# Modulations, weight splits, the experts' gate and the bias rows in a kernel of two stacked blocks

## The chip, the cores and the metric

The kernel runs on one core of one Trainium2 chip. The metric is the device time of one execution in microseconds, the median of the runs.

## The reference, cut to what matters

Two blocks run one after the other over 256 tokens of width 1024, in fp32. In the first block each of two layers takes six modulations (shift, scale and gate, twice) from a conditioning vector, the latent attention two more.

```python
# first block, per layer
sh1, sc1, g1, sh2, sc2, g2 = jnp.split(c_act @ w_mod[layer] + b_mod[layer], 6, axis=-1)
h = modulate(rmsnorm(x, norm_g[layer]), sh1, sc1)
x = x + g1 * mix(h)            # forgetting attention in layer 0, latent attention in layer 1
h = modulate(rmsnorm(x, ffn_norm_g[layer]), sh2, sc2)
x = x + g2 * grouped_moe(h)    # sum over e of combine[:, e] * (silu(h @ w_gate[e]) * (h @ w_up[e])) @ w_down[e]

# second block, four layers: retention, MoBA, differential, retention
x = x + mixer(_rmsnorm(x, norm1[i]))      # MoBA and differential add rel_bias[bucket(distance)] to the scores
u = jax.nn.relu(_rmsnorm(x, norm2[i]) @ w_up[i]); x = x + (u * u) @ w_down[i]
```

## The kernel before

Every product of a weight is made of three matmuls on a high and a low part. `unit` loads 1 MiB of a weight into one of five `raw` buffers (SP's queue, L136), and for each half ACT copies the high part `wh` (L149) and another engine subtracts it to get the low part `wl` (L155). Six half units of `wh` and `wl` exist at a time, so splits run at most six ahead of PE. The subtracting engine is DVE, but in the forgetting attention it is GpSimd (POOL) for all 34 half units, by `SPL`.

The stages follow each other: an opening (constants, the first two modulations), forgetting attention (44 to 236 us), experts of layer 0 (to 502), latent attention (to 690), experts of layer 1 (to 950), then the second block: retention, four perceptrons, MoBA, differential attention, and a second retention at the end. A scheduler orders the instructions of each engine by the order of the code and by what is ready; every engine then works its list in order. `issue_after` adds an edge on one engine, and `HOLD` uses it: after so many splits of a stage, further splits may not come ahead of the step in `last` on DVE. For the first retention it is 2.

A modulation is a product of the conditioning vector `c` with 1024x1024 of `w_mod`. It is done in four steps of a load and four DVE instructions each, one multiply (L813) or multiply-adds (L815), that accumulate 128 partial rows in `macc`, 512 columns wide; eight matmuls with ones (L826) sum the partitions. Two modulations belong to the opening, twelve are put into later stages: `spare()` takes steps from a queue at places in the code, their number set by `PLAN0`, `PLAN1` and `MF`.

An expert's output is gathered as `dv`, two parts again: ACT multiplies by the combine weight (L1398), DVE makes the low part (L1399), and PE spreads it back to the tokens (L1409). The gate is applied behind the last expert, four multiplies and four adds on DVE (L908, L909). Then `norm_x` takes the root mean square of `x` (squares on ACT, L278; root steps on DVE, L255 to L265; `diag`, L879), and every engine passes a branch (L1248) that isn't taken here.

The attentions of the second block read a relative bias from `bias_rows` in DRAM, sixteen heads of 128 equal rows of 384. `spread_bias` writes them with DMAs from DRAM to DRAM, four issues of four heads each on ACT's queue in the first retention, behind the second head's first square (L496, L590). In that stage `rv` (L469) and `rg` (L471) scale what PE has projected, on ACT.

Of the kernel before, what the change touches and what calls it, by code (L numbers as in the profile page):

```python
# [31 lines left out]
GE = 4  # L32
HOLD = dict(ret0=2, mlp0=2, mlp1=2, mlp2=2, mlp3=2, moba=4)
SPL = {'fgt': (1, 0)}
# [6 lines left out]
PLAN1 = [1, 1, 1, 3, 0, 0, 2, 0, 1, 1, 1, 1, 0, 2, 0, 2]  # L41
# [43 lines left out]
class Net:  # L85
    def __init__(self, ctx, tc, I, C, out):
# [5 lines left out]
        self.last = None  # L92
# [38 lines left out]
    def load(self, ap, k, n):  # L131
        raw = self.raw.tile([128, UNIT], F32, name="raw", tag="raw")
        rv = raw[:, :k * n].rearrange("p (k n) -> p k n", k=k)
        aps = [ap] if len(ap.shape) == 3 else [ap[:, m] for m in range(ap.shape[1])]
        for m, a in enumerate(aps):
            self.nc.sync.dma_start(rv[:, m * a.shape[1]:(m + 1) * a.shape[1]], a)  # L136
        return rv

    def unit(self, ap, k, n):
# [4 lines left out]
        for k0 in range(0, k, step):  # L144
# [4 lines left out]
            nc.scalar.copy(h[:, :m * n], p)  # L149
# [4 lines left out]
            with self.tc.issue_after(self.last) if self.last and self.nsplit > HOLD.get(self.ph, 99) else nullcontext():  # L154
# [113 lines left out]
    def rstd(self, srcs, n):  # L268
# [5 lines left out]
        for i, pieces in enumerate(srcs):  # L274
            for j, p in enumerate(pieces):
                junk = self.jk.tile([128, 512], F32, name="junk", tag="junk")
                w = p.shape[-1]
                nc.scalar.activation(junk[:, :w], p, AF.Square, scale=n ** -0.5, accum_out=ss[:, i, j:j + 1])  # L278
# [25 lines left out]
    def add_x(self, acc, scale=None):  # L304
# [9 lines left out]
        self.last = i.ins  # L314
# [17 lines left out]
    def heads(self, proj, mix, wo, gate=None):  # L332
# [5 lines left out]
        def add(xs, ps, g):  # L338
# [4 lines left out]
            self.last = nc.vector.tensor_tensor(xs, ps, xs, OP.add).ins  # L343
# [37 lines left out]
    def _mlp(self, i):  # L381
# [52 lines left out]
    def _retention(self, i, j):  # L434
# [41 lines left out]
        def mix(h, q, k, v, g):  # L476
# [11 lines left out]
            for tok in range(NT):  # L488
# [7 lines left out]
                mid = nc.scalar.activation(junk, po, AF.Square, scale=rt, accum_out=ss)  # L496
                if i == 0 and h == 1 and tok == 0:
                    with self.tc.issue_after(mid.ins):
                        self.spread_bias()
# [86 lines left out]
    def spread_bias(self):  # L586

        d = self.dist
        for g in range(4):
            self.nc.scalar.dma_start(self.bias[4 * g:4 * g + 4, :, 0:384],  # L590
                                     bass.AP(tensor=d.tensor, offset=d.offset + g * 4 * 384,
                                             ap=[[384, 4], [0, 128], [1, 384]]))
# [162 lines left out]

    def rope(self):
# [39 lines left out]

    def mod(self, w, c0, bias, gain=None):
# [6 lines left out]
        def step(u):  # L804
            half = u // 2
            r = self.load(self.rows(w, u % 2 * 4, 4, c0 + half * 512, 512), 4, 512)
            if u % 2 == 0:
                spot["acc"] = self.mods.tile([128, 512], F32, name="macc", tag="macc")
            acc = spot["acc"]
            for k in range(4):  # L810
                kk = u % 2 * 4 + k
                if kk == 0:
                    i = nc.vector.tensor_scalar(acc, r[:, k, :], self.c[:, 0:1], None, op0=OP.mult)  # L813
                else:
                    i = nc.vector.scalar_tensor_tensor(acc, r[:, k, :], self.c[:, kk:kk + 1], acc, op0=OP.mult,  # L815
                                                       op1=OP.add)
            with self.tc.issue_after(i.ins):
                self.finish()
            if u % 2:
                self.finish = lambda: total(acc, slice(4 * half, 4 * half + 4))  # L820

        def total(acc, c):
            self.finish = lambda: None
            ps = self.pat()
            for f in range(4):
                nc.tensor.matmul(ps[:, f:f + 1], acc[:, f * 128:f * 128 + 128], self.ones[:, 0:1], start=True, stop=True)  # L826
            self.mark = nc.vector.tensor_tensor(col[:, c], ps[:, 0:4], bias[:, c], OP.add).ins
            if gain is not None:
                nc.vector.scalar_tensor_tensor(col[:, c], col[:, c], 1.0, gain[:, c], op0=OP.add, op1=OP.mult)
# [3 lines left out]
    def gate(self, col):  # L833

        nc = self.nc
        self.finish()
# [5 lines left out]
        for half in range(2):  # L842
# [5 lines left out]
            nc.scalar.copy(g[:, half * 512:half * 512 + 512], ps)  # L848
        return g
# [767 lines left out]
```

## Time and profile before

| what | value |
|---|---|
| time, median of 3 runs | 2425.5 us (2424.55 to 2428.33) |
| time of the profiled execution | 2425.37 us |
| its span | 2423.6 us |
| PE busy | 2250.8 us (93%) |
| DVE busy | 1309.7 us (54%) |
| ACT busy | 990.5 us (41%) |
| POOL busy | 92.3 us (4%) |

The shares are means over stages with different limits. The line of 40 slices and the table by stretch tell which engine is full where, a wait names the instruction that an engine stood before and the one that it waited for, and the rows of a line give the price of one instruction. A row of an engine's sequencer (ACTq, SPq) shows the time that an issue of a DMA held its queue.

### The profile page before, as it was taken

To read this page: it belongs to the slowest core of one execution; us is meant where nothing else is said; L and a number is where in the kernel's file an instruction comes from. 1 tells how busy PE (TensorE), PEld (TensorE's weight loads), DVE (VectorE), ACT (ScalarE), POOL (GpSimd) and SP (SyncE) were. 2 spreads that over 40 slices of the span, in tenths; PEclk is the share of its full clock that TensorE was granted. 3 is DMA by queue.
4 is the path that set the end of the run, shared out by engine and by line. 5 is a ranking of instruction groups with operands and counts; after the bars stand their busy time and mean duration, and the time that the engine had idled before them with its cause. 6 is when DMAs were issued, how large, how long until landed. Compare 5 with 4: busy or idle time off the path is not lost.

```text
span 2423.6 us, 34244 instructions
## 1 busy us (share of the span) xinstructions
PE 2250.8 (93%) x13738; PEld 1769.9 (73%) x13738; DVE 1309.7 (54%) x2594; ACT 990.5 (41%) x1622; POOL 92.3 (4%) x46
## 2 busy tenths in 40 slices
PE   4898999969989997979999999999999999999999
PEld 3787443348964332868799898998888998787987
DVE  7867211178841113645655664655786556665554
ACT  3444211146631112434444465444574445443443
POOL 1443000000000000000000000000000000000000
PEclk9888999989989998989999999999999999999999
DMA  9767899966679996445555543655534555454552
GB/s 308 245 212 282 345 375 416 388 209 226 232 290 416 410 400 254 161 157 174 159 189 191 183 131 100 196 182 171 188 124 139 197 186 187 154 176 143 188 174 88
DMA packets 264391, 541.96 MB, mean 224 GB/s; under 512 B 15752, under 2 KB 158720, under 8 KB 250912
## 3 DMA queue, kind: packets, MB, share of 16 engines
q1 hardware_dynamic: 252208, 528.84, 61.6%
q10 hardware_dynamic: 12016, 10.85, 1.4%
q8 instruction: 111, 1.82, 0.3%
q14 instruction: 56, 0.46, 0.1%
HBM read 538.57 MB, written 4.22 MB: 224 GB/s over the span
## 4 chain that ended last, share of the span: by engine, by line
PE 52%; DVE 5%; ACT 1%; ACTq 1%; issue 1%; DMA 0%; DVEq 0%
DVE wl L155 2%; ACTq L590 1%; ACT wh L149 1%; DVE rsa L261 0%; DVE rsy L265 0%; DVE xg L217 0%; PE acc__mlp__19994 L201 0%; PE acc__mlp__13136 L201 0%; PE acc__mlp__16583 L199 0%; PE acc__mlp__13134 L201 0%; PE acc__mlp__19992 L201 0%; PE acc__mlp__9856 L200 0%; PE acc__mlp__16583 L200 0%; PE acc__mlp__9856 L199 0%; PE acc__mlp__19995 L200 0%
## 5 line engine op out<-in xcount | busy, mean ns | idle before, releaser
L155 DVE TENSOR_TENSOR wl<-raw,wh 128x1024 fp32r<-128x1024 f32 (+2 forms) x492 | 575.7, 1190 | 393.4 <-ACT wh L149 390.7
L149 ACT CAST wh<-raw 128x1024 fp32r<-128x1024 f32 (+4 forms) x526 | 523.3, 1020 | 472.2 <-issue 58.0
L815 DVE SCALAR_TENSOR_TENSOR macc<-raw,c,macc 128x512 f32<-128x512 f32 x196 | 169.7, 866 | 4.2 <-DMA raw<-in_w_mod_dram 1.5
L155 POOL TENSOR_TENSOR wl<-raw,wh 128x1024 fp32r<-128x1024 f32 (+1 forms) x34 | 82.0, 2435 | 136.5 <-ACT wh L149 136.5
L400 ACT CAST aTh<-rl 128x512 fp32r<-128x512 f32 x56 | 34.8, 621 | 78.3 <-DVE rl L398 78.3
L537 ACT ACTIVATE p<-p,m 128x128 f32<-128x128 f32 (+1 forms) x128 | 56.9, 447 | 23.1 <-DVE m L535 22.8
L278 ACT ACTIVATE junk<-x 128x512 f32<-128x512 f32 x52 | 32.7, 630 | 66.6 <-DVE x L343 36.5
L401 DVE TENSOR_TENSOR aTl<-rl,aTh 128x512 fp32r<-128x512 f32 x56 | 38.8, 693 | 38.5 <-ACT aTh L400 38.5
L398 DVE TENSOR_TENSOR rl<-rl 128x512 f32<-128x512 f32 x56 | 38.4, 685 | 0.0
L261 DVE SCALAR_TENSOR_TENSOR rsa<-rsy,rsh 128x1 f32<-128x1 f32 x186 | 34.4, 215 | 2.6
L220 ACT CAST hTh<-xg 128x512 fp32r<-128x512 f32 (+1 forms) x36 | 21.3, 606 | 25.7 <-DVE xg L217 25.6
L1173 POOL TENSOR_TENSOR hTl<-xg,hTh 128x512 fp32r<-128x512 f32 x8 | 10.1, 1278 | 471.1 <-ACT xg L1172 471.1
L265 DVE SCALAR_TENSOR_TENSOR rsy<-rsa,rsy 128x2 f32<-128x2 f32 (+2 forms) x141 | 22.6, 160 | 3.2
L537 ACT ACTIVATION_READ_ACCUMULATOR p<-p,m 128x1 f32 x128 | 24.1, 188 | 0.0
L221 DVE TENSOR_TENSOR hTl<-xg,hTh 128x512 fp32r<-128x512 f32 (+1 forms) x36 | 23.4, 671 | 1.0 <-ACT hTh L220 0.7
L1409 PEld LDWEIGHTS acc__moe__2360<-dv,back 64*128 64x128 f32 x32 | 5.6, 183 | 17.8 <-ACT dv L1398 10.4
L1409 PE MATMUL acc__moe__2360<-dv,back 64*128 64x512 f32 x32 | 14.8, 476 | 3.5 <-ACT dv L1398 3.2
L1409 PEld LDWEIGHTS acc__moe__6273<-dv,back 64*128 64x128 f32 x32 | 5.5, 183 | 16.6 <-ACT dv L1398 8.7
L1409 PE MATMUL acc__moe__6273<-dv,back 64*128 64x512 f32 x32 | 14.4, 476 | 2.8 <-ACT dv L1398 2.4
L535 DVE TENSOR_SCALAR m<-m 128x2 f32<-128x2 f32 x64 | 16.6, 259 | 0.5
L826 PE MATMUL at__latpre__4176<-ones,macc 128*128 128x1 f32 x8 | 1.8, 351 | 16.0 <-DVEq L1248 16.0
L813 DVE TENSOR_SCALAR macc<-raw,c 128x512 f32<-128x512 f32 x28 | 15.5, 553 | 1.5 <-DMA raw<-in_w_mod_dram 1.5
(3933 smaller groups left out, 7333.2 us busy)
## 6 DMA issues: line engine op xcount, KB each, us to landing
raw<-in_w_up_dram SPq DMA_DIRECT2D x64, 1024.0 KB, 5.4
raw<-in_w_down_dram SPq DMA_DIRECT2D x64, 1024.0 KB, 4.9
raw<-in_w_mod_dram SPq DMA_DIRECT2D x48, 1024.0 KB, 5.2
raw<-in_ret_w_in_dram SPq DMA_DIRECT2D x48, 1024.0 KB, 5.2
raw<-in_exp_w_gate_dram SPq DMA_DIRECT2D x40, 1024.0 KB, 10.3
raw<-in_exp_w_down_dram SPq DMA_DIRECT2D x34, 1024.0 KB, 9.9
raw<-in_exp_w_up_dram SPq DMA_DIRECT2D x30, 1024.0 KB, 10.5
wh<-in_exp_w_up_dram SPq DMA_DIRECT2D x34, 512.0 KB, 11.3
```

What stands on the lines that cost most here:

```text
L149: nc.scalar.copy(h[:, :m * n], p)
L155: eng.tensor_tensor(l[:, :m * n], p, h[:, :m * n].bitcast(F32), OP.subtract)
L221: nc.vector.tensor_tensor(lo[:, k0:k0 + n, tok * 128:tok * 128 + 128], pv, d.bitcast(F32), OP.subtract)
L261: nc.vector.scalar_tensor_tensor(a[:, c], y[:, c], h[:, c], y[:, c], op0=OP.mult, op1=OP.mult)
L278: nc.scalar.activation(junk[:, :w], p, AF.Square, scale=n ** -0.5, accum_out=ss[:, i, j:j + 1])
L398: nc.vector.tensor_tensor(rl, rl, rl, OP.mult)
L400: nc.scalar.copy(h, rl)
L401: nc.vector.tensor_tensor(aT[1][:, 2 * j:2 * j + 2, :].rearrange("p k t -> p (k t)"), rl, h.bitcast(F32), OP.subtract)
L537: nc.scalar.activation(p[:, m, :], p[:, m, :], AF.Exp, bias=mx[:, m:m + 1], accum_out=rs[:, m, s:s + 1])
L590: self.nc.scalar.dma_start(self.bias[4 * g:4 * g + 4, :, 0:384], bass.AP(tensor=d.tensor, offset=d.offset + g * 4 * 384, ap=[[384, 4], [0, ...
L815: i = nc.vector.scalar_tensor_tensor(acc, r[:, k, :], self.c[:, kk:kk + 1], acc, op0=OP.mult, op1=OP.add)
L1409: mm(acc[tok][half], back[c, e % 4, tok * 128:tok * 128 + 128], dv[j][c, :], start=e == 0 and j == 0, stop=e == 15 and j == 1)
```

## The change

1. Opening: each step of a modulation loads two rows of 1024 columns, PE multiplies them in four matmuls (into four quarters of the partitions), and DVE copies or adds one 128x512. Eight small matmuls with a constant `pick` sum up. The reordering of the queue goes.
2. Later modulations stay on DVE, 1024 columns wide: eight instructions each where there were sixteen.
3. `SPL` is empty: the 34 splits of the forgetting attention go to DVE.
4. `HOLD` becomes 0 for the first retention and is new, 0, for the latent stage. ACT's copies are held too, and `last` after `norm_x` is the pair of the last `diag` on DVE and the last square on ACT.
5. The gate is folded into each expert: DVE multiplies by combine weight and gate from PSUM, ACT copies the high part, DVE subtracts. The gate is laid out ahead of the first expert (`gate_halves`), and behind the last only four adds are left. `PLAN1` ends with 3 in place of 2.
6. `spread_bias` moves to the first perceptron, eight issues of two heads on SP's queue, each behind the newest weight load.

```diff
-GE = 4
-HOLD = dict(ret0=2, mlp0=2, ...)
-SPL = {'fgt': (1, 0)}
+HOLD = dict(ret0=0, latpre=0, mlp0=2, ...)
+SPL = {}
...
-            nc.scalar.copy(h[:, :m * n], p)
...
-            with self.tc.issue_after(self.last) if self.last and self.nsplit > HOLD.get(self.ph, 99) else nullcontext():
+            hold = self.last if self.nsplit > HOLD.get(self.ph, 99) else ()
+            with ExitStack() as e:
+                for i in hold:
+                    e.enter_context(self.tc.issue_after(i))
+                nc.scalar.copy(h[:, :m * n], p)
                 eng.tensor_tensor(l[:, :m * n], p, h[:, :m * n].bitcast(F32), OP.subtract)
...
             down(c, prev)
+            if i == 0:
+                with self.tc.issue_after(self.loaded):
+                    self.spread_bias(c)
...
-        for g in range(4):
-            self.nc.scalar.dma_start(self.bias[4 * g:4 * g + 4, :, 0:384],
...
+        self.nc.sync.dma_start(self.bias[2 * g:2 * g + 2, :, 0:384],
+                               bass.AP(tensor=d.tensor, offset=d.offset + g * 2 * 384, ap=[[384, 2], [0, 128], [1, 384]]))
...
+            r = self.load(self.rows(w, 2 * u, 2, c0, 1024), 2, 1024)
+            if u == 0:
+                spot["acc"] = self.mods.tile([128, 1024], F32, name="macc", tag="macc")
             acc = spot["acc"]
+            if side:
+                ps = self.pat()
+                for k in range(2):
+                    for half in range(2):
+                        j = 32 * (2 * k + half)
+                        nc.tensor.matmul(ps[j:j + 32, :], self.c[:, 2 * u + k:2 * u + k + 1].to_broadcast([128, 32]),
+                                         r[:, k, half * 512:half * 512 + 512], start=True, stop=True)
+                if u == 0:
+                    i = nc.vector.tensor_copy(acc[:, 0:512], ps)
                 else:
+                    i = nc.vector.tensor_tensor(acc[:, 0:512], ps, acc[:, 0:512], OP.add)
+            else:
+                for k in range(2):
...
+    def gate_halves(self, col):
...
+        g = self.mods.tile([128, D], F32, name="gate", tag="gate", bufs=1)[:, 0:512]
+        ps = self.pat()
+        for half in range(2):
+            for k in range(4):
+                kk = half * 4 + k
+                nc.tensor.matmul(ps[half * 64:half * 64 + 64, k * 128:k * 128 + 128],
+                                 self.ident[0:8, kk:kk + 1].to_broadcast([8, 64]), row, start=True, stop=True)
+        nc.scalar.copy(g, ps)
...
+        self.last = (i.ins, self.sq)
...
-            nc.scalar.mul(dv[0], ps, cs)
-            nc.vector.scalar_tensor_tensor(dv[1], ps, cs, dv[0].bitcast(F32), op0=OP.mult, op1=OP.subtract)
+            t = self.wk.tile([128, 512], F32, name="dg", tag="dg", bufs=1)
+            nc.vector.scalar_tensor_tensor(t, ps, cs, gates, op0=OP.mult, op1=OP.mult)
+            nc.scalar.copy(dv[0], t)
+            nc.vector.tensor_tensor(dv[1], t, dv[0].bitcast(F32), OP.subtract)
...
-        self.add_gated(acc, G)
+        self.add_x(acc)
         self.norm_x()
```

The first place is DVE's list behind the second layer's experts, where `x` has been added up, down to the branch. `var` to `rsy` are the root's steps, `wl` the first splits of the retention. Before, a part of it:

```order
L909 TENSOR_TENSOR x<-x,xg 128x512 x2
L155 TENSOR_TENSOR wl<-raw,wh 128x1024 x2
L281 SCALAR_TENSOR_TENSOR var<-ss 128x2
L155 TENSOR_TENSOR wl<-raw,wh 128x1024
L255 TENSOR_SCALAR rsy<-var 128x2
L257 TENSOR_SCALAR rsh<-var 128x2
L155 TENSOR_TENSOR wl<-raw,wh 128x1024
L256 TENSOR_SCALAR rsy<-rsy 128x2
L155 TENSOR_TENSOR wl<-raw,wh 128x1024
L261 SCALAR_TENSOR_TENSOR rsa<-rsy,rsh 128x1 x2
L155 TENSOR_TENSOR wl<-raw,wh 128x1024
```

After the change this chain holds no split; one stands behind `diag`, and the others behind the branch. The second root of the same stage, from which `rv` is made, then stands so on DVE:

```order
L157 TENSOR_TENSOR wl<-raw,wh 128x1024
L283 SCALAR_TENSOR_TENSOR var<-ss 128x2
L157 TENSOR_TENSOR wl<-raw,wh 128x1024
L257 TENSOR_SCALAR rsy<-var 128x2
L259 TENSOR_SCALAR rsh<-var 128x2
L157 TENSOR_TENSOR wl<-raw,wh 128x1024
L258 TENSOR_SCALAR rsy<-rsy 128x2
L157 TENSOR_TENSOR wl<-raw,wh 128x1024
L263 SCALAR_TENSOR_TENSOR rsa<-rsy,rsh 128x1 x2
L157 TENSOR_TENSOR wl<-raw,wh 128x1024
L267 SCALAR_TENSOR_TENSOR rsy<-rsa,rsy 128x2
L157 TENSOR_TENSOR wl<-raw,wh 128x1024
```

Six splits stand between `var` and the last step there, where two stood before.

The second place is the bias rows. Before, on ACT in the first retention, between a head's square and the next head's scaling:

```order
L149 CAST wh<-raw 128x1024 x5
L496 ACTIVATE junk,oss<-at__ret__8754,rsy 128x512
L590 DMA bias_rows<-bias_by_distance 512x1x384 x4
L469 ACTIVATE rv<-pj__ret__8837,rsy 128x512
L149 CAST wh<-raw 128x1024
```

After, on SP in the first perceptron, two of eight chunks:

```order
L135 DMA raw<-in_w_down_dram 128x2x1024 x2
L591 DMA bias_rows<-bias_by_distance 256x1x384
L135 DMA raw<-in_w_up_dram 128x8x256 x2
L135 DMA raw<-in_w_down_dram 128x2x1024 x2
L591 DMA bias_rows<-bias_by_distance 256x1x384
L135 DMA raw<-in_w_up_dram 128x8x256 x2
```

One issue now follows each pair of `w_down` loads, and the next pair of `w_up` loads is queued behind it.

The third place is DVE in the forgetting attention, between the first and the second group of heads (`o` and `aTl` are the first group's result, `b` the second group's decay). Before:

```order
L221 TENSOR_TENSOR aTl<-at__fgt__678,aTh 128x2x128
L827 TENSOR_TENSOR mod<-at__fgt__752,vcols 128x4
L813 TENSOR_SCALAR macc<-raw,c 128x512
L815 SCALAR_TENSOR_TENSOR macc<-raw,c,macc 128x512 x7
L827 TENSOR_TENSOR mod<-at__fgt__831,vcols 128x4
L813 TENSOR_SCALAR macc<-raw,c 128x512
L815 SCALAR_TENSOR_TENSOR macc<-raw,c,macc 128x512 x7
L827 TENSOR_TENSOR mod<-at__fgt__911,vcols 128x4
L813 TENSOR_SCALAR macc<-raw,c 128x512
```

After:

```order
L157 TENSOR_TENSOR wl<-raw,wh 128x1024
L568 TENSOR_TENSOR o<-at__fgt__668,rs 128x256
L833 SCALAR_TENSOR_TENSOR macc<-raw,c,macc 128x1024
L223 TENSOR_TENSOR aTl<-at__fgt__678,aTh 128x2x128
L850 TENSOR_TENSOR mod<-at__fgt__750,vcols 128x8
L157 TENSOR_TENSOR wl<-raw,wh 128x1024
L831 TENSOR_SCALAR macc<-raw,c 128x1024
L833 SCALAR_TENSOR_TENSOR macc<-raw,c,macc 128x1024 x5
L850 TENSOR_TENSOR mod<-at__fgt__898,vcols 128x8
L833 SCALAR_TENSOR_TENSOR macc<-raw,c,macc 128x1024
```

The splits stand among the modulations' instructions now, where POOL had a list of its own; fewer and wider instructions accumulate the modulations.

## Rows read from the trace of the kernel before

**Rows 1.** The page's line of PE's busy tenths in 40 slices of the span.

```profile
PE   4898999969989997979999999999999999999999
```

**Rows 2.** Table by stretch: us, busy us and instructions by engine, clock, DMA share, GB/s.

```profile
15.00:43.00 28.00, 7.83 (x33) 7.25 (x34) 23.59 (x42) 1.99 (x2) 2.92 (x2) 1.00 1.06 374
60.00:240.00 180.00, 156.50 (x1179) 146.66 (x1179) 137.77 (x291) 77.37 (x162) 71.68 (x31) 0.87 0.71 243
```

**Rows 3.** Opening, DVE: a group (busy, mean ns), then the timeline (start, us).

```profile
L815 DVE SCALAR_TENSOR_TENSOR macc<-raw,c,macc 128x512 f32<-128x512 f32 x28 | 21.0, 751 | 2.3 <-DMA raw<-in_w_mod_dram 1.5
...
14.90 0.49 DVE L813 TENSOR_SCALAR macc<-raw,c 128x512 f32<-128x512 f32 x1 [1.09 <-DMA raw<-in_w_mod_dram]
37.49 3.12 DVE L815 SCALAR_TENSOR_TENSOR macc<-raw,c,macc 128x512 f32<-128x512 f32 x4
```

**Rows 4.** Groups: splits (whole span), multiply-adds at 43:240 and 300:500, final norm.

```profile
L155 POOL TENSOR_TENSOR wl<-raw,wh 128x1024 fp32r<-128x1024 f32 (+1 forms) x34 | 82.0, 2435 | 136.5 <-ACT wh L149 136.5
L155 DVE TENSOR_TENSOR wl<-raw,wh 128x1024 fp32r<-128x1024 f32 (+2 forms) x492 | 575.7, 1190 | 393.4 <-ACT wh L149 390.7
L815 DVE SCALAR_TENSOR_TENSOR macc<-raw,c,macc 128x512 f32<-128x512 f32 x84 | 86.2, 1026 | 1.5
L815 DVE SCALAR_TENSOR_TENSOR macc<-raw,c,macc 128x512 f32<-128x512 f32 x10 | 7.5, 747 | 0.2
L1510 DVE SCALAR_TENSOR_TENSOR x<-x,rx,gf 128x1024 f32<-128x1024 f32 x2 | 2.6, 1283 | 0.3 <-DMA gf<-in_final_norm_g_dram 0.3
```

**Rows 5.** PE's waits, 43 to 240 us: total us, times, longest.

```profile
PE at__fgt__503 L957 <- DVE lf L955: 2.9, 1, 2.9
...
PE pj__fgt__1062 L184 <- POOL wl L155: 1.6, 1, 1.6
```

**Rows 6.** Behind layer 0's experts, 500 to 519 us: PE's wait, DVE's groups.

```profile
PE at__latpre__4176 L826 <- DVEq L1248: 16.0, 1, 16.0
...
L815 DVE SCALAR_TENSOR_TENSOR macc<-raw,c,macc 128x512 f32<-128x512 f32 x10 | 7.4, 745 | 0.0
L155 DVE TENSOR_TENSOR wl<-raw,wh 128x864 fp32r<-128x864 f32 (+1 forms) x4 | 3.0, 752 | 0.0
...
L908 DVE TENSOR_TENSOR xg<-acc__moe__2360,gate 128x512 f32<-128x512 f32 x1 | 0.7, 691 | 0.0
```

**Rows 7.** Behind layer 1's experts: PE's wait, and the second root's end on DVE.

```profile
PE at__ret__8051 L214 <- DVEq L1248: 14.1, 1, 14.1
...
980.95 0.15 DVE L265 SCALAR_TENSOR_TENSOR rsy<-rsa,rsy 128x2 f32<-128x2 f32 x1
```

**Rows 8.** First retention: ACT's timeline, PE's wait, stretch, DMA queue, three heads' L479.

```profile
1051.76 18.44 ACTq L590 DMA_DIRECT2D bias_rows<-bias_by_distance  x3
...
PE pj__ret__8909 L171 <- ACT rv L469: 11.4, 1, 11.4
...
1063.00:1077.00 14.00, 6.01 (x15) 4.76 (x16) 4.96 (x12) 6.19 (x9) 0.00 (x0) 0.52 0.27 90
...
q10 hardware_dynamic: 1980, 3.02, 19.4%
...
L479 PE MATMUL at__ret__8399<-rot x4: 379/379/483, 1008.1 to 1008.9; 128*128 128x256 f32 x4
L479 PE MATMUL at__ret__8744<-rot x4: 379/379/483, 1047.2 to 1047.9; 128*128 128x256 f32 x4
L479 PE MATMUL at__ret__9093<-rot x4: 379/379/483, 1104.0 to 1104.7; 128*128 128x256 f32 x4
```

**Rows 9.** First perceptron: SP's and ACT's timeline; the page's landing times.

```profile
1238.29 6.13 SPq L136 DMA_DIRECT2D raw<-in_w_up_dram  x2
1260.94 6.13 SPq L136 DMA_DIRECT2D raw<-in_w_up_dram  x2
...
1257.16 1.05 ACT L149 CAST wh<-raw 128x1024 fp32r<-128x1024 f32 x1 [2.39 <-issue]
...
raw<-in_w_up_dram SPq DMA_DIRECT2D x64, 1024.0 KB, 5.4
```

More of the change, by code (lines that the diff above doesn't have):

```diff
@@ L342, in add @@
                 ps = t
-            self.last = nc.vector.tensor_tensor(xs, ps, xs, OP.add).ins
+            self.last = (nc.vector.tensor_tensor(xs, ps, xs, OP.add).ins,)
         cur = proj(0)
@@ L495, in mix @@
                 junk = self.jk.tile([128, 512], F32, name="junk", tag="junk")
[L496 to L499, printed above, removed]
+                nc.scalar.activation(junk, po, AF.Square, scale=rt, accum_out=ss)
                 nc.vector.tensor_scalar(ss, ss, 1.0 / 512, EPS, op0=OP.mult, op1=OP.add)
@@ L754, in prepare @@
         nc.vector.memset(self.ones, 1.0)
+        self.pick = self.b1.tile([128, 2], F32, name="pick", tag="pick")
+        nc.vector.memset(self.pick, 0.0)
+        for j in range(4):
+            nc.vector.memset(self.pick[32 * j:32 * j + 1, j % 2:j % 2 + 1], 1.0)
     def rope(self):
@@ L804, in step @@
         def step(u):
[L805 to L808, printed above, removed]
+            side = self.ph == "start"
+            r = self.load(self.rows(w, 2 * u, 2, c0, 1024), 2, 1024)
+            if u == 0:
+                spot["acc"] = self.mods.tile([128, 1024], F32, name="macc", tag="macc")
             acc = spot["acc"]
[L810 to L813, printed above, removed]
-                else:
-                    i = nc.vector.scalar_tensor_tensor(acc, r[:, k, :], self.c[:, kk:kk + 1], acc, op0=OP.mult,
-                                                       op1=OP.add)
+            if side:
[7 more added lines that the diff above has]
+                    i = nc.vector.tensor_copy(acc[:, 0:512], ps)
+                else:
+                    i = nc.vector.tensor_tensor(acc[:, 0:512], ps, acc[:, 0:512], OP.add)
+            else:
+                for k in range(2):
+                    kk = 2 * u + k
+                    if kk == 0:
+                        i = nc.vector.tensor_scalar(acc, r[:, k, :], self.c[:, 0:1], None, op0=OP.mult)
+                    else:
+                        i = nc.vector.scalar_tensor_tensor(acc, r[:, k, :], self.c[:, kk:kk + 1], acc, op0=OP.mult,
+                                                           op1=OP.add)
@@ L817, in step, with total @@
             with self.tc.issue_after(i.ins):
                 self.finish()
-            if u % 2:
-                self.finish = lambda: total(acc, slice(4 * half, 4 * half + 4))
-        def total(acc, c):
+            if u == 3:
+                self.finish = lambda: total(acc, side)
+        def total(acc, side):
             self.finish = lambda: None
             ps = self.pat()
-            for f in range(4):
-                nc.tensor.matmul(ps[:, f:f + 1], acc[:, f * 128:f * 128 + 128], self.ones[:, 0:1], start=True, stop=True)
-            self.mark = nc.vector.tensor_tensor(col[:, c], ps[:, 0:4], bias[:, c], OP.add).ins
+            for f in range(8):
+                if side:
+                    nc.tensor.matmul(ps[:, f:f + 1], acc[:, f % 4 * 128:f % 4 * 128 + 128],
+                                     self.pick[:, f // 4:f // 4 + 1], start=True, stop=True)
+                else:
+                    nc.tensor.matmul(ps[:, f:f + 1], acc[:, f * 128:f * 128 + 128], self.ones[:, 0:1], start=True,
+                                     stop=True)
+            self.mark = nc.vector.tensor_tensor(col, ps[:, 0:8], bias, OP.add).ins
@@ L900, in modnorm @@
         return hT
-    def add_gated(self, acc, G):
-        nc, x = self.nc, self.x
-        for tok in range(NT):
-            for half in range(2):
-                c = slice(half * 512, half * 512 + 512)
-                t = self.cm.tile([128, 512], F32, name="xg", tag="xg")
-                nc.vector.tensor_tensor(t, acc[tok][half], G[:, c], OP.mult)
-                self.last = nc.vector.tensor_tensor(x[:, tok, c], x[:, tok, c], t, OP.add).ins
     def forgetting(self, A, SH, G):
```

44 lines of the change are left out of this document (25 added, 19 removed).

## The prediction, made before the changed kernel ran

> **What bounds the kernel now.** The busy line in 40 slices comes first [rows 1]: from slice 18 on, about 1080 us, PE is at 9 and nothing but less PE work or an end to a PE stall can shorten that half. Ahead of it PE has gaps and a clock under full speed, so that is where to look, and the table by stretch says what fills it [rows 2]. In 15 to 43 us PE is busy for 7.83 of 28 us and the DMA share reads 1.06. In 60 to 240 us, the forgetting attention, PE has 156.50 of 180 us at a clock of 0.87, with DVE at 137.77 and POOL at 71.68. Then I read what PE waits for, stretch by stretch: at the ends of the two expert stages it stands for 16.0 and 14.1 us while DVE works [rows 6, 7], in the first retention for 11.4 us [rows 8]. The terms follow in the order of time. The profiled run took 2425.37 us, the median is 2425.5: I add the sum to 2425.4.
>
> **The opening: -4 (-7 to -1).** All waits there lead to the last macc on DVE: 28 multiply-adds of 751 ns and 4 multiplies of 0.49 us are 23 us for 8 loads, 2.87 us each [rows 3]. The change does them as four matmuls and one 128x512 copy or add per load, about 0.7 us of DVE by the gate multiply of that size [rows 6], so the loads themselves come last. At 374 GB/s [rows 2] a 1 MiB load takes 2.80 us, nearly what DVE took: there is little slower about DVE than about DMA. The gain is that the modulation loads stand first in the queue and no longer wait for buffers: the first macc began at 14.90 us and the last four ended at 40.6 [rows 3]; 14.9 + 7 x 2.80 = 34.5, then four matmuls and an add, about 2 us, so 36.5 against 40.6, -4.1. The weights of the first projection then land behind them, which bounds the gain: if PE waits for these, only 1 us is left.
>
> **Forgetting attention: -8 (-28 to +12).** 34 splits leave POOL, where one took 2435 ns, for DVE, where one takes 1190 ns: +40.5 us on DVE [rows 4]. The modulations go to rows twice as wide: 84 multiply-adds, 86.2 us, and 12 multiplies, 0.49 each [rows 3] or 5.9, become 42 and 6. For 128x1024 the nearest row is the final norm's multiply at 1283 ns, for the 6 I take 0.8: 53.9 + 4.8 = 58.7 against 92.1, so -33.4. That works because the 128x512 multiply-add takes 1026 ns here and 747 in the expert stage where POOL makes no splits [rows 4]. DVE's load therefore stays at about 145 of 180 us, or less where small operations also lose their stretching, and the splits get 1.2 us shorter. What can come back is what PE waits for: DVE's lf for 2.9 us, the longest, and wl on POOL for 1.6 [rows 5]. The eight waits of that list that end on DVE sum to 14.1 us and the two that end on POOL to 2.5, 16.6 together. Against it stands order: DVE works its list in order, and in the new one a run of six 128x1024 multiply-adds, 7.5 us, stands between two splits and the next scores, where POOL split by itself before. I take half of 16.6. The low end is all 16.6 and half of the clock's loss (0.13 x 180 = 23): -28. The high end is nothing back, and in each of four head groups one split that comes 3 us late: +12.
>
> **Experts and the way out of them: +1 and -3.5.** The gate moves into the product: multiply from PSUM on DVE, copy on ACT, subtract on DVE, one step longer than now (0.7 us by the gate multiply of the same size [rows 6]). Only the last expert of each layer shows it, where PE has nothing else to do until dv comes: 2 x 0.7 = 1.4, and the gate's copies are now half as long, so I take +1. Behind it the branch holds PE 16.0 us [rows 6]. DVE works through 10 multiply-adds (7.4 us), four splits (3.0), and four gate multiplies of 0.7 [rows 6]. The change leaves one split (1.0), no gate multiplies and four wide multiply-adds (4 x 1.28, 5.1): 2.0 + 2.8 + 2.3 = 7 us less work. About half shows, for the squares on ACT and the dependent steps of the root, now covered by these, stand bare: -3.5 (-5.5 to 0).
>
> **Modulations in the latent stage: -1 (-3 to +2).** Six modulations lie there and in the expert stages; each goes from 14 x 0.75 + 2 x 0.49 = 11.5 us to 7 x 1.28 + 0.8 = 9.8, so 10 us less on an engine that PE seldom waits for there.
>
> **Second way out, into the first retention: +2 (-3 to +6).** Here PE waits 14.1 us for the branch [rows 7]. Six splits stand before it, 7.1 us at 1190 ns [rows 4], and four gate multiplies, 2.7. Five splits go behind the branch (6.0 us), so the branch falls some 5 us earlier. But they come out again in the next chain on DVE: the value scale rv needs a second root, whose last step is at 980.95 [rows 7], and PE takes up its product right behind. In the new order six splits stand inside that chain where two stood, and two of these need buffers that PE frees only near the end of its first projection; 4 x 1.2 = 4.8 eats the 5, and buffer waits cost about 2.
>
> **The bias rows: -17.7 (-18 to -14).** In the first retention four DMA issues sit on ACT's queue, 18.44 us for the last three, and rv for the next head waits behind them; PE waits 11.4 us, and from 1063 to 1077 its granted clock is 0.52, near the lower of its two levels, 1.2 GHz [rows 8]. The heads run the same code: from the first head's L479 to the second's 1047.2 - 1008.1 = 39.1 us, to the third's, over the issues, 1104.0 - 1047.2 = 56.8. The difference, 17.7, is the price of the issues with their clock. They go to SP in the first perceptron, one of half the size in each of eight chunks, behind the newest weight load. There the chunk's period is 1260.94 - 1238.29 = 22.65 us, and four 1 MiB loads go out in it; an up load issued at 1238.29 needs 5.4 us and is cast at 1257.16 [rows 9], so 13.5 us of delay cost nothing. The four old transfers are 3.02 MB, at 90 GB/s 33.6 us, 8.4 each [rows 8]; a new one is half of that, 4.2 us at the same rate and 8.4 at half of it. Both are under 13.5, also as time that SP itself is held: cost 0. The bias is first read in the stage behind.
>
> While the rows were spread before, the DMA share was 0.27 with 90 GB/s [rows 8], about four of sixteen engines, for an outer dimension of four. The Trainium skill (DMA: Bandwidth & Descriptors, "Why a DMA increments its semaphore by 16 and not by 1") says that the largest number of engines up to 16 that divides the slowest dimensions is used; this agrees with the row. By it the new shape, an outer dimension of two, has two engines, and the transfer takes the longer 8.4 us. It speaks against the change; the sum stays as it is by either value, and only the next part's chance hangs on it.
>
> **The sum.** -4 - 8 + 1 - 3.5 - 1 + 2 - 17.7 = -31.2: 2394 us.
>
> **Rivals.**
> *Slower: the spread chokes the perceptron's loads.* Few of the sixteen engines carry it, and every weight load has to pass these too. Four loads by 2.80 us hold each engine for 11.2 of the 22.65 us, which leaves 11.5 for the transfer. If it takes T, more than that, each of eight chunks runs late by T - 11.5, less the slack of 13.5 us once. At T = 18 that is 8 x 6.5 - 13.5 = 38.5, and from there on the kernel is slower than before; at T = 21, 2.5 times the 8.4, it is 62.5: 2456.5. Against it stands the row (8.4 is under 11.5), for it only that no row shows such a transfer mixed with loads: 0.04.
> *DVE becomes the bound of the attention.* The high end, +12 instead of -8: 2414. For it: the run of wide instructions between splits, and DVE at 137.77 already. Against it: the stretching by POOL goes. 0.17.
> *The attention gives all back, clock included:* -28 instead of -8: 2374. For it: the clock of 0.87 follows PE's gaps. 0.17.
> *The held splits don't do what they say:* the chains stay bound by squares and loads, 0 for the first way out and +6 for the second, and the opening -1: 2394 + 3.5 + 4 + 3 = 2404.5. 0.12.
> My forecast, 2384 to 2402, has the remaining 0.50.
>
> **How the numbers follow.** The range takes in the neighbours, 2374 and 2414, and on the low side a few us of the small terms: 2367 to 2415. It leaves out the choked loads and the corners where several ends meet, about 0.2 together. A measurement of this kernel tells about 0.2% (5 us) from no change. Slower is the choke, with a small share of an attention worse than +12: 0.05. Same needs -31 to shrink to less than 5, all high ends at once: 0.03. Faster: 0.92.
>
> **What would show it.** In the profile after: no DMA issue on ACT between two heads, and 39 us from the second L479 to the third; if it stays above 45, the issues weren't the cause. SP's issues in the first perceptron hold it under 13 us and PE stays at 9; a wait of ACT for a weight load there is the first rival. No POOL split, multiply-adds of 128x1024 near 1.28 us in the attention, and PE's waits for DVE under 10 us in all; more than 20 us for wl on DVE is the second rival. PE's wait at the branch near 12.5 and 9 us, with rv late after the second. The prediction is wrong if the time to the first expert stage falls by less than 5 us or by more than 30.

## The result, and the profile after

The changed kernel takes 2382.6 us, the median of 4 runs (2378.57 to 2383.23), against 2425.03 in the same comparison: a ratio of 0.9818, 95% interval 0.9806 to 0.983. That is 42.4 us less, where 31.2 were forecast. The two profiled executions, spans of 2423.6 and 2381.4 us, are compared by stage below; a stage begins with its first matmul in the trace. By this measure the attention of the kernel before ends at 230.7 us and its latent stage at 682.7.

| stage | before, us | after, us | difference | forecast |
|---|---|---|---|---|
| opening, to the attention's first matmul | 43.9 | 42.1 | -1.8 | -4 |
| forgetting attention | 186.8 | 162.2 | -24.6 | -8 |
| experts, layer 0 | 272.0 | 276.3 | +4.3 | +0.5 |
| way out to the latent stage | 16.0 | 9.3 | -6.7 | -3.5 |
| latent attention | 164.0 | 165.1 | +1.1 | -1 |
| experts, layer 1 | 267.5 | 268.0 | +0.5 | +0.5 |
| way out and first retention | 239.3 | 221.4 | -17.9 | +2 - 17.7 |
| first perceptron | 187.6 | 187.6 | 0 | 0 |
| the rest | 1040.5 | 1043.3 | +2.8 | 0 |

One trace tells a stage only so far. In the kernels of the experiments below whose code for a stage is that of the changed kernel, the opening took 40.7 to 44.3 us, the attention 163.0 to 164.7, the experts of layer 0 275.2 to 279.6, the latent stage 163.3 to 167.8 and the rest 1041.1 to 1044.8. A second trace of the stages as they were before (the first experiment) took 44.1 for the opening, 274.3 for the experts of layer 0 and 1042.6 for the rest. So the attention's gain is 22 to 25 us, and the differences of the opening, the latent stage and the rest lie within what a stage varies by itself.

PE's busy tenths on the page after, as [rows 1]:

```profile
PE   6998999979989997999999998999999999999998
```

The 18th slice, 7 before, held the stall of the first retention and reads 9; the 16th, which holds the way out in front of that stage, stays at 7, and the right half is as full as it was (the 25th and the last read 8 for 9).

The table by stretch (us, busy us by engine with instructions, clock, DMA share, GB/s), of the whole attention stage. Before, then after:

```profile
44.00:231.00 187.00, 166.34 (x1236) 155.97 (x1237) 147.17 (x282) 83.13 (x172) 78.11 (x33) 0.88 0.71 240
```

```profile
42.00:204.50 162.50, 156.31 (x1228) 149.18 (x1228) 132.09 (x259) 82.90 (x173) 0.00 (x0) 0.91 0.82 280
```

PE's idle time falls from 20.7 to 6.2 us and its busy time by 10.0, of nearly the same matmuls (1236 and 1228 in the trace) at a higher granted clock. DVE, which took over all splits of POOL, is busy for 15 us less. The groups of DVE there (busy, mean ns, idle before and its releaser) say why, beside [rows 4]:

```profile
L833 DVE SCALAR_TENSOR_TENSOR macc<-raw,c,macc 128x1024 f32<-128x1024 f32 x42 | 53.7, 1277 | 0.3
L157 DVE TENSOR_TENSOR wl<-raw,wh 128x1024 fp32r<-128x1024 f32 (+1 forms) x34 | 38.8, 1155 | 2.3 <-ACT wh L156 2.3
...
L537 DVE TENSOR_SCALAR m<-m 128x2 f32<-128x2 f32 x16 | 2.6, 164 | 0.0
```

All waits of PE from 40 to 212 us, as [rows 5] (total, times, longest):

```profile
PE pj__fgt__347 L184 <- ACT wh L156: 3.0, 1, 3.0
PE at__fgt__957 L549 <- ACT p L539: 2.4, 2, 2.1
PE pj__fgt__1167 L184 <- ACT wh L156: 0.4, 1, 0.4
PE acc__moe__2089 L1181 <- DVE xg L343: 0.3, 1, 0.3
PE pj__fgt__416 L184 <- ACT wh L156: 0.3, 1, 0.3
```

PE waits for no split on DVE, and of its 14.1 us of waits for DVE 0.3 are left. The first line is new: the first weights land and are cast later than the modulations are ready.

At the two ways out (as [rows 6, 7]) PE waits less for the branch, but then for the second root's product:

```profile
PE at__latpre__4147 L848 <- DVEq L1283: 9.3, 1, 9.3
PE acc__moe__2303 L1447 <- ACT dv L1436: 3.1, 2, 1.6
...
PE at__ret__8008 L216 <- DVEq L1283: 7.8, 1, 7.8
PE pj__ret__8172 L173 <- ACT rv L474: 4.4, 1, 4.4
```

In the first retention (as [rows 8]) the third head's scores start 39.0 us after the second's, where they took 56.8; the bias rows on SP (ns, minimum, median, maximum of an issue) hold it 0.6 us each:

```profile
L484 PE MATMUL at__ret__8701<-rot x4: 379/379/483, 1019.8 to 1020.5; 128*128 128x256 f32 x4
L484 PE MATMUL at__ret__9046<-rot x4: 379/379/483, 1058.8 to 1059.6; 128*128 128x256 f32 x4
```

```profile
L591 SPq DMA_DIRECT2D bias_rows<-bias_by_distance x8: 599/600/754, 1137.5 to 1289.9; - x8
```

### The profile page after: what moved, and what is told of

It reads as the page before. It is cut to its first block, busy times and chain, and to the rows that moved or that the text cites. A ratio compares the mean times of both kernels' runs of the same rounds, so it can differ in the third digit from the quotient of the medians.

```text
span 2381.4 us, 34230 instructions
## 1 busy us (share of the span) xinstructions
PE 2255.3 (95%) x13802; PEld 1763.2 (74%) x13802; DVE 1285.7 (54%) x2518; ACT 986.2 (41%) x1620; POOL 10.3 (0%) x12
## 4 chain that ended last, share of the span: by engine, by line
PE 53%; DVE 5%; ACT 1%; issue 1%; DMA 1%; ACTq 0%; SPq 0%; DVEq 0%
DVE wl L157 2%; ACT wh L156 1%; DVE rsa L263 0%; DVE rsy L267 0%; PE acc__mlp__13096 L201 0%; PE acc__mlp__19954 L201 0%; PE acc__mlp__9809 L201 0%; PE acc__mlp__13097 L201 0%; PE acc__mlp__16544 L202 0%; PE acc__mlp__19955 L201 0%; PE acc__mlp__16544 L201 0%; PE acc__mlp__9810 L203 0%; PE acc__mlp__13096 L202 0%; PE acc__mlp__19955 L203 0%; PE acc__mlp__9810 L201 0%
## 5 line engine op out<-in xcount | busy, mean ns | idle before, releaser
L157 DVE TENSOR_TENSOR wl<-raw,wh 128x1024 fp32r<-128x1024 f32 (+4 forms) x526 | 614.7, 1188 | 379.4 <-ACT wh L156 375.8
L833 DVE SCALAR_TENSOR_TENSOR macc<-raw,c,macc 128x1024 f32<-128x1024 f32 x84 | 107.4, 1278 | 0.4
L1436 ACT CAST dv<-dg 128x512 fp32r<-128x512 f32 x32 | 19.8, 618 | 102.4 <-DVE dg L1435 102.4
L403 DVE TENSOR_TENSOR aTl<-rl,aTh 128x512 fp32r<-128x512 f32 x56 | 38.8, 692 | 38.5 <-ACT aTh L402 38.5
L1437 DVE TENSOR_TENSOR dv<-dg,dv 128x512 fp32r<-128x512 f32 x32 | 22.1, 691 | 18.3 <-ACT dv L1436 18.3
L1447 PE MATMUL acc__moe__2303<-dv,back 64*128 64x512 f32 x32 | 15.2, 494 | 9.3 <-ACT dv L1436 8.3
L1447 PE MATMUL acc__moe__6191<-dv,back 64*128 64x512 f32 x32 | 14.3, 477 | 7.0 <-ACT dv L1436 6.5
L1447 PE MATMUL acc__moe__2304<-dv,back 64*128 64x512 f32 x32 | 15.4, 497 | 0.0
L1447 PE MATMUL acc__moe__6192<-dv,back 64*128 64x512 f32 x32 | 14.3, 477 | 0.0
```

The costliest lines, as they stand in the source:

```text
L157: eng.tensor_tensor(l[:, :m * n], p, h[:, :m * n].bitcast(F32), OP.subtract)
L403: nc.vector.tensor_tensor(aT[1][:, 2 * j:2 * j + 2, :].rearrange("p k t -> p (k t)"), rl, h.bitcast(F32), OP.subtract)
L1447: mm(acc[tok][half], back[c, e % 4, tok * 128:tok * 128 + 128], dv[j][c, :], start=e == 0 and j == 0, stop=e == 15 and j == 1)
```

## The experiments

**The splits of the attention, alone.** The kernel before with one line changed, and the changed kernel with that line undone, one run each.

```diff
-SPL = {'fgt': (1, 0)}
+SPL = {}
```

> The kernel before with one edit: the 34 splits of the forgetting attention go to DVE, the modulations stay 512 columns wide. Theory A (POOL's splits stretch whatever DVE does beside them, and that stretch is what PE waited for): the multiply-add of 128x512 falls from 1026 to about 750 ns in the attention, and the stage from 187 us (44 to 231) to about 170, so the kernel to about 2408. Theory B (the gain came from the wider modulations): the stage stays at 187 or grows, since DVE gets 40 us of splits, and the kernel stays at 2425 or above.

> The changed kernel with the 34 splits of the attention on POOL again, all else as changed. Theory A: the multiply-adds of 128x1024 stretch from 1278 ns to about 1700 or more, the small operations with them, and the stage grows from 162 us (42 to 204.5) to at least 180; the kernel to about 2400. Theory B: the stage stays near 165, the kernel near 2385.

They took 2412.87 and 2402.19 us. The attention's length in the four combinations:

| modulations | splits on POOL | splits on DVE |
|---|---|---|
| 512 wide | 186.8 (before) | 168.1 |
| 1024 wide, opening on PE | 177.5 | 162.2 (after) |

DVE's groups in the attention (busy, mean ns, idle before), first of the kernel before with the splits on DVE, then of the changed one with the splits on POOL:

```profile
L815 DVE SCALAR_TENSOR_TENSOR macc<-raw,c,macc 128x512 f32<-128x512 f32 x82 | 60.3, 743 | 0.5
```

```profile
L833 DVE SCALAR_TENSOR_TENSOR macc<-raw,c,macc 128x1024 f32<-128x1024 f32 x42 | 73.3, 1745 | 0.5
...
L537 DVE TENSOR_SCALAR m<-m 128x2 f32<-128x2 f32 x16 | 7.5, 469 | 0.1
```

Theory A holds, with both numbers near its own (750 and over 1700 ns): moving the splits is worth 15 to 19 us of the stage, the wider modulations (with the opening) 6 to 9; with 163.0 to 164.7 in place of the single 162.2 these are 13 to 19 and 3 to 9. The opening has little part in it: with the opening back on DVE (the last experiment) the attention took 163.0. Theory B falls. That POOL is simply the slower splitter is not enough either: PE waited for its splits for 2.5 us in the kernel before. The second stage came to 177.5 where 180 was the least expected.

**The held splits in the first retention.** HOLD back to 2, and then one more edge:

```diff
-HOLD = dict(ret0=0,
+HOLD = dict(ret0=2,
```

> The changed kernel with HOLD of the first retention at 2 again, so that splits stand in front of the branch as before. If the held splits give back at the second root what they gain at the branch: the first retention starts about 3 us later (the splits are now the only ones there, the gate multiplies are gone), rv comes earlier by as much, and the kernel stays at 2382 within 2 us. If the early branch is a gain that lasts: 2386 or more.

```diff
             hold = self.last if self.nsplit > HOLD.get(self.ph, 99) else ()
+            if self.ph == "ret0" and self.nsplit > 4:
+                hold = (self.root, self.sq0)
```

Here `root` is the last step of the second root on DVE, `sq0` its last square on ACT.

> The changed kernel with one more edge: in the first retention the splits past the first four wait for the second root on DVE, and their high parts for its last square on ACT. If the six splits inside that root are what makes rv late (PE waits 4.4 us for it): the root takes 2 us in place of 8, PE's wait for rv goes, and the kernel is 3 to 5 us faster than the changed one, 2378. Rival: PE then waits for the low parts of the next unit instead, and nothing is won (2382).

HOLD at 2 took 2382.98 us (2381.49 to 2389.72), ratio 0.9831 (0.9807 to 0.9855): as the changed kernel. Its way out is 8.6 us in place of 7.8, the stage behind it 212.2 in place of 213.6. `last` is still the pair behind `norm_x`, so two splits come into the chain in front of the branch, where six stood in the kernel before: this undoes the change for the first two only. The sum of both stages is 220.8 and 221.4, no difference. The second edge took 2376.89 us (2373.53 to 2377.79), 0.9796 (0.9777 to 0.9814), each run below each of the changed kernel, and its first retention 207.5 us, 6.1 less. Together with the kernel below that has this edge too (late spreading back, no different in time) it is the fastest here. On DVE the second root then reads (start, us):

```profile
945.13 0.15 DVE L286 SCALAR_TENSOR_TENSOR var<-ss 128x2 f32<-128x2 f32 x1
...
947.26 0.16 DVE L269 SCALAR_TENSOR_TENSOR rsy<-rsa,rsy 128x2 f32<-128x2 f32 x1
947.37 3.50 DVE L159 TENSOR_TENSOR wl<-raw,wh 128x1024 fp32r<-128x1024 f32 x3
```

In the changed kernel the same steps ran from 943.70 to 952.12:

```profile
943.70 0.16 DVE L283 SCALAR_TENSOR_TENSOR var<-ss 128x2 f32<-128x2 f32 x1
943.77 1.23 DVE L157 TENSOR_TENSOR wl<-raw,wh 128x1024 fp32r<-128x1024 f32 x1
...
951.96 0.16 DVE L267 SCALAR_TENSOR_TENSOR rsy<-rsa,rsy 128x2 f32<-128x2 f32 x1
```

2.3 us against 8.4. PE's wait for rv is gone, and none for a low part took its place: the rival falls.

**The gate.** The changed kernel with the gate behind the experts again:

```diff
-            nc.vector.scalar_tensor_tensor(t, ps, cs, gates, op0=OP.mult, op1=OP.mult)
-            nc.scalar.copy(dv[0], t)
-            nc.vector.tensor_tensor(dv[1], t, dv[0].bitcast(F32), OP.subtract)
+            nc.scalar.mul(dv[0], ps, cs)
+            nc.vector.scalar_tensor_tensor(dv[1], ps, cs, dv[0].bitcast(F32), op0=OP.mult, op1=OP.subtract)
...
-        self.add_x(acc)
+        self.add_gated(acc, G)
```

> The changed kernel with the gate applied behind the last expert again: ACT multiplies by the combine weight, DVE makes the low part, four multiplies more behind the experts. Theory C (folding costs what PE waits for dv: 8.3 us in layer 0's experts and 6.5 in layer 1's against 3.2 and 2.4 before): the experts get 4 to 5 us shorter in layer 0 and up to 4 in layer 1, the two branches 2.5 us later each, and the kernel ends within 3 us of the changed one, on either side. Rival (the experts are bound by their loads, so dv's waits cost nothing and the fold is a gain): the kernel is 4 us slower, 2387.

2389.23 us (2385.62 to 2391.42), 0.9853 (0.9836 to 0.9869): 6.6 us slower than the changed kernel, each run above each of its runs, so folding is a gain, and theory C's total (within 3 us) is missed. The profiled execution was the fastest of the four (2385.62), so the table of stages shows only part of the 6.6. By stage both are half right: the experts take 272.9 and 264.4 us, 3.4 and 3.6 less, as C said, while the ways out take 16.9 and 10.0, 7.6 and 2.2 more. PE's longest waits from 200 to 500 us:

```profile
PE at__latpre__4108 L848 <- DVEq L1292: 16.9, 1, 16.9
...
PE acc__moe__2303 L1454 <- ACT dv L1443: 3.2, 4, 0.8
```

So with the splits held and the gate behind, the first way out is no shorter than before (16.0). The order of DVE changed with it: five wide multiply-adds and a multiply stand between the last add of `x` and `diag`, where the changed kernel has one and a multiply; the four more are 5.1 us at 1.28. How the 6.7 us part between gate, splits and modulations is therefore not settled.

**Late spreading back.** The changed kernel with the further edge in the first retention, and in the experts the spreading back of an expert's output moved behind the next expert's down product:

> The changed kernel with the splits held behind the second root in the first retention, and in the experts with the spreading back of an expert's output put behind the next expert's down product. If PE's waits for dv (8.3 and 6.5 us) are what folding costs: they fall under 3 us in each layer, the experts get 3 us shorter each, the tails stay, and the kernel comes to 2371, about 5 us under the one with the held splits alone. Rival (the experts are bound by loads): they stay at 276 and 268 us, 2377.

```diff
-            if dv is not None:
-                put_back(e - 1, dv)
             next(steps, None)
-            dv = down(e, sg)
+            new = down(e, sg)
+            if dv is not None:
+                put_back(e - 1, dv)
+            dv = new
```

2374.7 us (2372.55 to 2375.95), 0.9795 (0.9781 to 0.9808): no different from 0.9796 with the held splits alone. The waits for dv didn't fall, so the edit didn't do what it was made for:

```profile
PE acc__moe__2303 L1451 <- ACT dv L1440: 8.5, 8, 1.6
```

Still layer 0's experts took 272.1 us against 275.2, and layer 1's 267.7 against 266.6. What the 4.3 us of layer 0 are stays open: the waits for dv alone aren't it, and two traces of the same experts before the change lie 2.3 apart.

**The bias rows.** Three kernels, one run each, issue nothing in the perceptron and four transfers on ACT in the first retention: back to back, as before; back to back with the 128 rows as the outer dimension; and one behind each head. The first cut shows the place of the first two, the second how the issue of the second differs from that of the other two:

```diff
+                if i == 0 and h == 1 and tok == 0:
+                    with self.tc.issue_after(mid.ins):
+                        for b in range(4):
+                            self.spread_bias(b)
...
-        self.nc.scalar.dma_start(self.bias[4 * g:4 * g + 4, :, 0:384],
-                                 bass.AP(tensor=d.tensor, offset=d.offset + g * 4 * 384, ap=[[384, 4], [0, 128], [1, 384]]))
+        self.nc.scalar.dma_start(self.bias[4 * g:4 * g + 4, :, 0:384].rearrange("h r c -> r h c"),
+                                 bass.AP(tensor=d.tensor, offset=d.offset + g * 4 * 384, ap=[[0, 128], [384, 4], [1, 384]]))
```

> The changed kernel with the four issues of the bias rows back to back on ACT's queue behind the second head's square, as before, and none in the perceptron. If the whole price was there: the second head to the third takes 56.8 us again in place of 39, the kernel is 17.7 us slower, 2400. If the perceptron pays part of it now: the first perceptron gets shorter by that part.

> As the one with four issues on ACT, but each written with the 128 rows as the outer dimension, so that the transfer has 128 in place of 4 there. Theory D (ACT was held because four engines took 39 us over the rows, and the queue took a new issue only when the last had drained): the transfer spreads over all engines, 768 KB need some 2 to 3 us, ACT is held for under 8 us in all and the second head to the third takes 39 to 45 us; the kernel about 2385. Rival E (an issue of 512 rows costs ACT 8 us by itself): held for 18 us as before, 56 us, 2400.

> The changed kernel with the four issues on ACT in the first retention, one behind each head's first square, in the old shape of four outer rows. Theory D: each finds an empty queue and holds ACT for 1.2 to 1.4 us, as the first two did; each head takes 39 to 41 us, the kernel is 1 to 5 us slower than the changed one. Rival E: each holds ACT for 8 us or more, and each head takes several us longer, 2395 or above.

| kernel | us | second head to third | first retention |
|---|---|---|---|
| changed | 2382.6 | 39.0 | 213.6 |
| four on ACT, as before | 2405.91 | 55.7 | 230.1 |
| four on ACT, 128 outer rows | 2386.41 | 38.8 | 214.2 |
| one per head on ACT | 2381.79 | 39.1 | 213.5 |

ACT's queue in the three (start, us; in the first two, the three issues behind the first one):

```profile
1028.86 18.91 ACTq L592 DMA_DIRECT2D bias_rows<-bias_by_distance  x3
```

```profile
1025.83 2.06 ACTq L592 DMA_DIRECT2D bias_rows<-bias_by_distance  x3
```

```profile
983.62 1.22 ACTq L591 DMA_DIRECT2D bias_rows<-bias_by_distance  x1
1022.71 0.64 ACTq L591 DMA_DIRECT2D bias_rows<-bias_by_distance  x1
1061.79 0.61 ACTq L591 DMA_DIRECT2D bias_rows<-bias_by_distance  x1
1109.36 0.60 ACTq L591 DMA_DIRECT2D bias_rows<-bias_by_distance  x1
```

Theory E falls: the four issues hold ACT for 20.1, 2.7 or 3.1 us in all. So what cost was neither an issue as such nor ACT as its place, but issues right behind each other with four outer rows. One detail of theory D doesn't come out, that the queue takes a new issue only when the last has drained. In the first kernel the four took 1.22, 1.78, 8.45 and 8.61 us, so the second was taken while the first still ran and only the later ones waited, each for about one transfer; in the second kernel all four were taken in 2.7 us, while their rows lay over 14.6 us. The perceptron without the rows is no shorter: 190.1, 190.2 and 187.6 us in the three, against 187.6. The total of the first run, 23 us more, is above the 16.5 of its stage; the rest lies in small differences of other stages. One issue per head is as fast as the changed kernel, where 1 to 5 us more were expected.

**The choke.** Each of the eight transfers three times, and all eight in one chunk, one run each:

```diff
-                    self.spread_bias(c)
+                    for _ in range(3):
+                        self.spread_bias(c)
```

> The changed kernel with each of the eight bias transfers in the perceptron issued three times over, on the same queue. One transfer's packets took 8.6 us in the changed kernel, on two engines by their count and length. If a load has to pass these engines in order behind them: they hold 26 us and the loads 11.2 of a period of 22.65 us, each chunk runs some 14.5 us late, less 13.5 of slack once: the perceptron takes 187.6 + 8 x 14.5 - 13.5, about 290 us, the kernel about 2485. Rival (the loads don't wait behind the spread on those engines): the perceptron stays under 195.

```diff
-            if i == 0:
+            if i == 0 and c == 1:
                 with self.tc.issue_after(self.loaded):
-                    self.spread_bias(c)
+                    for b in range(8):
+                        self.spread_bias(b)
```

> The changed kernel with the eight bias transfers issued one behind the other in the second chunk of the perceptron, in place of one per chunk; the bytes, the shape and the queue are the same. If loads have to pass the two engines behind the transfers: these are busy for 8 x 8.6 = 69 us, the next loads land some 69 us later, 13.5 of it is slack, and the perceptron takes 187.6 + 55 = 243 us, the kernel 2437. Rival (the queue or the engines take loads past the transfers): the perceptron stays under 195, and one issue per chunk was not needed.

The first took 2493.26 us, its perceptron 294.6 where the sum gave 290. But the repeats write what the one before wrote, and SP itself waited for that:

```profile
SPq L592 <- DMA bias_rows<-bias_by_distance: 159.1, 16, 18.1
```

So its number agrees by another mechanism, and it doesn't tell. The second has no such wait and took 2425.99 us, as much as the kernel before the change; its perceptron is 227.3 us, 39.7 longer where 55 was expected. SP's queue, then the waits of ACT and PE, then a table row (clock, DMA share, GB/s at the end):

```profile
1168.72 56.97 SPq L592 DMA_DIRECT2D bias_rows<-bias_by_distance  x8
```

```profile
ACT wh L156 <- DMA raw<-in_w_up_dram: 48.2, 1, 48.2
...
PE pj__mlp__10368 L184 <- ACT wh L156: 36.0, 1, 36.0
```

```profile
1190.00:1230.00 40.00, 21.43 (x134) 18.97 (x132) 6.22 (x7) 3.86 (x5) 0.00 (x0) 0.79 0.14 45
```

The transfers hold the queue for 57 us, and the next load is issued behind them. So the loads came late because SP could not issue them; whether a load that is already issued also waits on those engines, as the expectation had it, is not shown apart. 45 GB/s at a share of 0.14 is half of the rate in [rows 8], as for two engines of sixteen, and in the changed kernel the packets of one transfer lie over 8.6 us. One per chunk is what makes them free. The rule of the Trainium skill (DMA: Bandwidth & Descriptors, "Why a DMA increments its semaphore by 16 and not by 1") said two engines for an outer dimension of two, four for four; these rates agree, and so does the short hold with 128 outer rows above.

**The opening.** The changed kernel with its two first modulations on DVE, 1024 wide:

```diff
-            side = self.ph == "start"
+            side = False
```

> The changed kernel with the opening's two modulations on DVE (1024 columns wide) in place of PE. If PE's opening is worth what the first stage shows: the attention starts at 44 us in place of 42.1, and the kernel is 1 to 3 us slower than the changed one, 2385. Rival (the opening is bound by its loads, and DVE was no slower): the same start within 0.5 us and the same time. Further possibility: the attention behind it gains or loses because PE was at work before it; then its length differs from 162 us by more than 3.

2387.81 us, one run. The attention starts at 44.2 us in place of 42.1 and takes 163.0. But the opening on PE took 40.7 to 44.3 us in the other kernels, 42.4 in the mean, and of the 5 us in the total 2.5 lie in the first perceptron, whose code is the same. So a gain of about 2 us is likely, and the rival (no gain) is not excluded.

## Why the prediction was right, and where it was off

The direction, the range and the largest certain term came out: 2382.6 lies in 2367 to 2415, and the time to the first expert stage fell by 26.4 us, between the 5 and the 30 that would have been a sign against it. It is just under 2384 to 2402, the forecast itself. That the sum is only 11 us off has some luck in it: the attention gave 16.6 us more than forecast, the two ways out (the second with the bias rows) 5.4 more, and the opening, the experts of layer 0, the latent stage and the rest took back 10.9. What came in the attention is nearest to the rival in which it gives all back, clock included (0.17).

1. **The bias rows** (-17.7, measured between the second and the third head): right to 0.1 us, and the perceptron paid 0, as forecast. Comparing two heads of the same code priced a stall with the clock that follows it. That the transfer takes 8.4 us at half the rate was right too: its packets lie over 8.6 us in the trace. The slower rival did not come. The run with all eight at once shows that narrow transfers can stop the loads, though by holding the queue that issues them: there the kernel was back at 2426.
2. **The attention** is the term that was mis-sized: -8 was forecast and -24.6 measured, near the low end of -28. The step that failed is the choice of half of PE's 16.6 us of waits. Nearly all came back: of the waits for DVE and POOL 0.3 us are left, and PE's idle time fell by 14.5, with 3.0 of a new wait in it. With them came 10 us of busy time as the granted clock rose from 0.88 to 0.91, while I had put that at the far end. The fear for which I halved it, a run of wide multiply-adds between two splits, has no wait of PE for a low part behind it in the trace. The share of each part stands in the two-by-two table.
3. **The opening**, -4 forecast and -1.8 measured, went as its lower bound said: PE waits 3.0 us for the first weights, which land behind the modulations. By the spread of this stage the size is not known better than to 2 us.
4. **The second way out**: +2 forecast and about 0 measured (-17.9 in all, less the -17.7). The mechanism was the one described: the branch came 6.3 us earlier, the second root gave it back, and the run with one more edge took 6.1 us out again. The 2 us for buffers, which no row had shown, did not come: in the trace after the six splits and the root's steps follow each other without a gap.
5. **The first way out** gave -6.7 where -3.5 was forecast: the wait at the branch was put near 12.5 and read 9.3. I had counted on half of the removed 7 us of work to show, and nearly all of it did; which part of the change that is owed to stays open, as said under the gate.
6. **The experts**: +4.3 in layer 0, of which the spread of the stage leaves 1 to 8. I had let only the last expert pay for the longer chain; PE's waits for dv rose from 3.2 to 8.3 us over eight places. The runs don't show that these waits are the 4.3, and the kernel with the gate behind has 3.4 less in that stage; this step was too optimistic, and its cause is not settled.
7. **The latent stage and the rest**: -1 was forecast for the one and +1.1 measured, 0 for the other and +2.8. The instructions of DVE and ACT in the rest are the same, one by one, and both differences are within the spread above, so nothing is shown there, and a gain of 1 us could not have been seen.

## What to carry to other kernels

Before work is moved off an engine to relieve another, look whether the two slow each other: a mean duration that differs between stages for the same instruction and shape is the sign, and the move back can be cheaper than the durations say. Before a small difference of a stage is explained, look at the same stage in traces where its code is the same. Splits or other fill work that is held behind one chain comes out in the next; hold it behind the last chain that PE waits for. Price a stall by the distance of two repetitions of the same code, with and without it, since that has the clock in it, and put small transfers on few engines one at a time, far enough apart that the last has drained.

## What the runs showed of the hardware that I had not expected

- A 128x1024 multiply-add on DVE takes 1277 ns alone and 1745 in the mean with POOL's splits beside it, a 128x2 multiply 164 and 469. Two single 128x32 ones took 185 ns alone and 2394 there, as long as a whole split on POOL (2435 in the kernel before). So small ones lose most for their length, and the 128x2 ones stand between the scores and PE's next product with them. Not every instruction is stretched: the 128x256 ones that make `p` from the scores took 421 ns alone and 406 to 423 there.
- The time that an issue holds its queue is not its own: 768 KB in 512 rows took 0.6 to 1.2 us where the one before had drained, and three of them 18.44 to 18.91 right behind another with four outer rows, the last two 8.35 to 8.61 each. With 128 outer rows three took 2.06 us, though the rows of all four were still under way for 13 us more.
- Transfers on two engines, 45 GB/s, held SP's queue, and with it the next weight loads, for 57 us, while the DMA share was 0.14.
